# Block two's table products and their transfers at the end of a down projection instead of in the feed-forward loop

## The chip, the cores and the metric

The kernel runs on one core of a Trainium2 chip. The metric is the device time of one execution in microseconds; lower is better. Three runs of the kernel before gave 1399.70, 1400.94 and 1398.84 us, median 1399.7.

## What is computed

Two transformer blocks of two layers each run over one sequence of 256 positions and 1024 features, all in float32. Block one mixes by a gated recurrence (HGRN2) and by sparse attention (NSA), then a gated feed-forward. Block two mixes by attention with a relative bias, then a feed-forward with a convolution of width 3 over the positions. Cut to what the change touches:

```
def first_block(x, ...):
    for l in range(DEPTH):
        ...
        x = layer_norm(ALPHA * x + mix, ln1_g[l], ln1_b[l])
        ffn = (jax.nn.silu(x @ w_ffn_gate[l]) * (x @ w_ffn_up[l])) @ w_ffn_down[l]
        x = layer_norm(ALPHA * x + ffn, ln2_g[l], ln2_b[l])
    return x

def conv_ffn(h, w_up, conv_w, conv_b, w_down):
    u = h @ w_up
    up = jnp.pad(u, ((0, 0), (CONV_WIDTH - 1, 0), (0, 0)))
    c = conv_b
    for j in range(CONV_WIDTH):
        c = c + conv_w[j] * up[:, j:j + S]
    ...

def second_block(x, ..., rel_bias, ...):
    table_a = rel_bias[:, :A_HEADS].T
    table_b = rel_bias[:, A_HEADS:A_HEADS + B_HEADS].T
    for layer in range(DEPTH):
        h = rmsnorm(x, attn_norm[layer])
        ...
        l_own = jnp.where(d_own >= 0, l_own + table_hk[:, t5_bucket_2(d_own)], -jnp.inf)
        ...
        x = x + conv_ffn(h, w_up[layer], conv_w[layer], conv_b[layer], w_down[layer])
```

The moved step prepares two things for block two: the convolution's weights and bias with the features on partitions, and the relative bias laid out by distance.

## The kernel before

The 256 positions are two token blocks of 128 ("tb" 0 and 1). A weight is loaded by SyncE (SP) into one of four buffers "raw", 512 KB at a time; ScalarE (ACT) rounds it into "whi" (line 122), and VectorE (DVE) or GpSimd (POOL) writes the rest, "wlo" (line 128). A product is three matmuls: high with high, high with low, low with high (`mm3`, line 137; line 135 is every matmul, line 143 every transpose). PSUM has eight banks under four names: acc 3, S 2, T 2, O 1.

Each engine does its instructions strictly in its own order. That order is not the one in which the code is written: a planner orders what the code records, by the recorded place as priority and by what is ready on its own estimate of time, and `issue_after` and `high_priority` bend it. SP and POOL also have their transfers in this order: an issue that must wait holds up what stands behind it on the same engine.

`block2_tables` (line 487) is the moved step. For each layer of block two it loads the three taps and the bias of the convolution (44 rows) into a tile "sg", transposes them by four matmuls into PSUM and evacuates them into "taps". Then `rel_rows` (line 174) does, for "ev" (the first layer of block two) and "od" (the second):

- SP loads `c_rel` (33 x 384) into "sg"; one product gives the bias of 16 heads by distance; ACT evacuates it into another "sg" tile;
- POOL writes that row to HBM, "relrow" (line 190, 24 KB), waits until it has landed, and issues four copies "relrep" (line 196), each of which repeats the rows of four heads 128 times, 768 KB.

The tag "sg" has two buffers, which the feed-forward loop uses too. `load_bias` (line 208) later reads "relrep" into the tables tb2a and tb2b, at the start of each layer of block two.

`layer1` (line 499) is a layer of block one. Its feed-forward loop (line 554) runs over eleven column groups of 256, and has the moved step in front of the fifth group of the second layer. Then `proj_out` (line 294) does the down projection. At its end the second token block's last products stand, and a last piece of them, `rest`, is kept back for `handover` (line 403): the seam to block two. There the layer norm and the RMS norm of token block 0 run on DVE, ACT and POOL (`layer_norm` line 333, `rms_rows` line 857); TensorE (PE) transposes the normalised rows ("xn", eight transposes into two S banks), does `rest` and the first products of block two for token block 0, and then the same again for token block 1. Each norm takes its reciprocal root "rs" from POOL (`rsqrt`, line 145). The weights of the seam are w_in_even; the second half of them, for the T banks, goes into the tiles "hT", where POOL subtracts every other piece.

Of the kernel before, what the change touches and what calls it, by code (L numbers as in the profile page):

```python
# [18 lines left out]
P = 128  # L19
S = 256  # L20
# [4 lines left out]
NF = D_FF // P  # L25
# [58 lines left out]
class Kern:  # L84
# [86 lines left out]
            sl = slice(k * 512, k * 512 + 512)  # L171
            self.nc.sync.dma_start(self.x[:, tb, sl], self.I["x"][0, tb * P:(tb + 1) * P, sl])

    def rel_rows(self, stage, small, names):

        nc, I = self.nc, self.I
        for name in names:
            key, nh, c0, w = {"b1": ("rel_bias", 8, 0, 384), "ev": ("rel_bias_2", 16, 0, 384),
                              "od": ("rel_bias_2", 16, 384, 384), "cmp": ("rel_bias", 8, 768, 512)}[name]
            rb = self.t(self.small, (33, 16), tag="rb", bufs=2)  # L180
            nc.gpsimd.memset(rb[32:33, :nh], 1.0)
            nc.sync.dma_start(rb[0:32, :nh], I[key])
            rel = stage((33, 512))
            nc.sync.dma_start(rel[:, :w], I["c_rel"][:, c0:c0 + w])
            ps = self.psum("T")
            self.mm(ps[:nh, :w], rb[:, :nh], rel[:, :w])
            sb = small((16, 512))
            self.act(sb[:nh, :w], ps[:nh, :w])
            dr = self.dram.tile([nh, w], F32, name="relrow_" + name)
            nc.gpsimd.dma_start(dr, sb[:nh, :w])  # L190

            reps = 15 if name == "cmp" else P
            dd = self.dram.tile([nh, reps, w], F32, name="relrep_" + name)
            ap = dr[:, :]
            for h in range(0, nh, 4):
                nc.gpsimd.dma_start(dd[h:h + 4], bass.AP(tensor=ap.tensor, offset=ap.offset + h * w, ap=[[w, 4], [0, reps], [1, w]]))
            self.relrow[name] = dd
# [289 lines left out]
    def block2_tables(self, fp):  # L487
        nc, I = self.nc, self.I
        for l in range(2):
            raw = self.t(fp, (2 * NF, 4, P), tag="sg", bufs=2)  # L490
            nc.sync.dma_start(raw[:, 0:3, :], I["conv_w_2"][l].rearrange("j (m p) -> m j p", p=P))
            nc.sync.dma_start(raw[:, 3, :], I["conv_b_2"][l].rearrange("(m p) -> m p", p=P))
            ps = self.psum("T", (P, 4, 2 * NF))
            for j in range(4):
                self.tr(ps[:, j, :], raw[:, j, :], 2 * NF)
            self.act(self.taps[:, l], ps)
        self.rel_rows(lambda sh: self.t(fp, sh, tag="sg", bufs=2), lambda sh: self.t(fp, sh, tag="sg", bufs=2), ("ev", "od"))

    def layer1(self, l, xT, accs):
        nc, I, tc = self.nc, self.I, self.tc  # L500
        w = I["w_in"][l]
        mix = self.new_xT()
        with ExitStack() as st:
            hp = st.enter_context(tc.tile_pool(name="hg", bufs=1))
            self.pl = 0.5
            vv = self.t(hp, (P, 2, 512), tag="hv")
            for tb in range(2):
                self.act(vv[:, tb, :], accs[0][tb])
            fps = self.proj_a(w, 512, 512, xT)
            pcs = [self.wpiece(w[:, j * S:(j + 1) * S], NK, S, self.pl) for j in range(2)]  # L510
            lf, kk = self.hgrn_gates(l, fps, hp)
            qT = self.hgrn_q(w, xT, hp, pcs)
            kT = self.t(hp, (P, 4, S), tag="hkT")
            for tb in range(2):
                ps = self.psum("T", (P, 4, P))
                for h in range(4):
                    self.tr(ps[:, h, :], kk[:, tb, h * P:(h + 1) * P])
                nc.vector.tensor_copy(kT[:, :, tb * P:(tb + 1) * P], ps)
            if l == 0:
                self.hgrn_tables(hp)  # L520
            scs = [self.hgrn_scores(h, lf, kT, qT, hp) for h in range(4)]
            if l == 0:
                self.nsa_tables(hp)
            kv = self.nsa_keys(l, w, xT, hp)
            G = self.hgrn_g(l, w, xT, hp)
            for h in range(4):
                self.hgrn_out(l, h, scs[h], vv, G, mix, hp)
            nq = self.nsa_queries(w, xT, hp)
            self.nsa_attn(nq, kv, mix, hp)
            rows = [self.row(hp, I[key][l], D, tag) for key, tag in (("ln1_g", "lfh"), ("ln1_b", "lfl"))]  # L530
            self.pl = 0.5
            slots = self.slot_pairs(hp, [("hE", 2, 2)] * 2 + [(tag, 1, None) for tag in ("hkT", "hqT", "hv", "hG")])
            accs, rest = self.proj_out(I["w_out"][l], lambda k: (mix[0][:, k, :], mix[1][:, k, :]), [[0, 1, 2, 3], [4, 5, 6, 7]], slots)
            xT, (ga,) = self.handover(lambda tb: self.layer_norm(tb, accs[tb], rows), self.x, I["w_ffn_gate"][l],
                                      [(0, "acc", None)], rest)
            self.D(f"xa_{l}", self.x)
        with ExitStack() as st:
            fp = st.enter_context(tc.tile_pool(name="ffn", bufs=1))
            self.pl = 0.0
            rows = [self.row(fp, I[key][l], D, key) for key in ("ln2_g", "ln2_b")]  # L540
            hT = self.hidden(fp)

            ua = self.proj_a(I["w_ffn_up"][l], 0, 512, xT, "S")
            for tb in range(2):
                sg = self.t(fp, (P, 512), tag="sg", bufs=2)
                with tc.issue_after(self.after[0].ins):
                    self.act(sg, ga[tb], AF.Silu)
                nc.vector.tensor_tensor(sg, sg, ua[tb], ALU.mult)
                ps = self.psum("T", (P, 4, P))
                for k in range(4):  # L550
                    self.tr(ps[:, k, :], sg[:, k * P:(k + 1) * P])
                for c in range(2):
                    self.split(*[h[:, :, tb * P:(tb + 1) * P] for h in hT[c]], ps[:, 2 * c:2 * c + 2, :])
            for c in range(2, NF // 2):
                if l == 1 and c == 4:
                    self.block2_tables(fp)
                accs = []
                for key, tag in (("w_ffn_gate", "acc"), ("w_ffn_up", "S")):
                    accs.append(self.proj_b(I[key][l], c * S, S, xT, tag))
                sg = self.t(fp, (P, 2, S), tag="sg", bufs=2)  # L560
                self.act(sg, accs[0], AF.Silu)
                nc.vector.tensor_tensor(sg, sg, accs[1], ALU.mult)
                self.split(*hT[c], sg)
            args = self.hidden_args(fp, hT)
            self.pl = 0.0
            accs, rest = self.proj_out(I["w_ffn_down"][l], *args)
            norm = lambda tb: self.layer_norm(tb, accs[tb], rows)
            if l == 0:
                return self.handover(norm, self.x, I["w_in"][1], [(1024, "acc", None)], rest)
            return self.rms(fp, norm, I["attn_norm_2"][0], I["w_in_even_2"][0],  # L570
                            [(1024, "acc", None), (2560, "T", args[2])], rest)
# [535 lines left out]
```

## Time and profile before

| | before |
|---|---|
| median of 3 runs | 1399.7 us (1398.84 to 1400.94) |
| the profiled execution's own time | 1399.82 us |
| its span, first to last instruction | 1398.0 us |
| instructions | 24398 |
| busy: PE, PE weight loads, DVE, ACT, POOL | 98%, 87%, 70%, 58%, 21% |
| mean granted clock of PE | 0.993 of full speed |
| moved by DMA | 243.27 MB, mean 174 GB/s |

A profile is one execution. Its page gives the busy time of each engine and the chain of work that ended last. The trace behind it can be asked for a stretch: the instructions in order of time with the wait in front of each, the busy time of every engine by stretch, and the landing times of transfers. "<-" stands between what an instruction writes and reads. A row with x4 is four instructions that follow each other. The clock of PE is given as a share of 2.4 GHz.

### The profile page before, as it was taken

The page shows a single profiled execution, that of the slowest core. Times are in us where ns is not written, and L with a number is a line of the kernel's source. Part 1 is how long each engine was busy: PE and PEld are TensorE (multiplying, and loading weights), DVE is VectorE, ACT ScalarE, POOL GpSimd, SP SyncE. Part 2 cuts the span into 40 slices and gives each one's busy share as a digit, 9 for nine tenths or more (in the row PEclk, how much of TensorE's full clock was granted, in tenths as well). Part 3 has the DMA queues.
Part 4 walks back from the last instruction along what each step waited for, and adds up shares of the span by engine and source line. Part 5 has one row for each costly group of instructions (what it writes and reads, how often), then busy time and mean ns, then how long its engine had stood idle before and what let it go on. Part 6 is the DMA issues. An engine that isn't in the chain of part 4 may idle for free. (4 is left out here: it accounts for less than half of the span.)

```text
span 1398.0 us, 24398 instructions
## 1 busy us (share of the span) xinstructions
PE 1364.3 (98%) x8873; PEld 1210.2 (87%) x8873; DVE 979.7 (70%) x2006; ACT 813.9 (58%) x1623; POOL 299.8 (21%) x308
## 2 busy tenths in 40 slices
PE   8999999999999999999998998999999999999998
PEld 7788689998788967999887997799988988899986
DVE  5579675554877877655476699678866666688864
ACT  5466645554475574555454676577655577676653
POOL 3265210000234532020014545200001323100000
PEclk9999999999999999999999999999999999999999
DMA  8564155665655434689564654266556744456552
GB/s 267 159 208 151 61 180 170 184 187 170 198 151 172 121 106 131 206 242 292 181 210 136 222 150 152 78 195 190 187 183 200 240 144 155 153 172 184 186 187 100
DMA packets 188923, 243.27 MB, mean 174 GB/s; under 512 B 15551, under 2 KB 133346, under 8 KB 188803
## 3 DMA queue, kind: packets, MB, share of 16 engines
q1 hardware_dynamic: 179987, 228.22, 52.8%
q0 software_dynamic: 8816, 13.50, 2.9%
q8 instruction: 70, 1.15, 0.3%
q14 instruction: 50, 0.41, 0.1%
HBM read 240.49 MB, written 9.24 MB: 179 GB/s over the span
## 5 line engine op out<-in xcount | busy, mean ns | idle before, releaser
L128 DVE TENSOR_TENSOR wlo<-raw,whi 128x512 fp32r<-128x512 f32 (+2 forms) x619 | 458.3, 752 | 265.7 <-ACT whi L122 199.7
L122 ACT ACTIVATE whi<-raw 128x512 fp32r<-128x512 f32 (+1 forms) x742 | 454.6, 626 | 317.8 <-PE T L135 90.5
L128 POOL TENSOR_TENSOR wlo<-raw,whi 128x512 fp32r<-128x512 f32 (+2 forms) x123 | 172.0, 1403 | 656.3 <-ACT whi L122 654.9
L135 PE MATMUL acc<-xhi,whi 128*128 128x256 f32 x1048 | 298.2, 285 | 5.3 <-ACT whi L122 5.3
L135 PE MATMUL acc<-xlo,whi 128*128 128x256 f32 x1048 | 298.4, 285 | 0.0
L135 PE MATMUL acc<-xhi,wlo 128*128 128x256 f32 x1048 | 298.2, 285 | 0.0
L135 PEld LDWEIGHTS acc<-xhi,whi 128*128 128x128 f32 x1048 | 200.9, 192 | 7.7 <-ACT whi L122 5.9
L135 PEld LDWEIGHTS acc<-xhi,wlo 128*128 128x128 f32 x1048 | 200.8, 192 | 1.9 <-issue 0.6
L135 PEld LDWEIGHTS acc<-xlo,whi 128*128 128x128 f32 x1048 | 201.0, 192 | 1.5 <-issue 0.2
L135 PE MATMUL S<-xhi,whi 128*128 128x256 f32 x608 | 172.2, 283 | 0.0
L135 PE MATMUL S<-xlo,whi 128*128 128x256 f32 x608 | 172.2, 283 | 0.0
L135 PE MATMUL S<-xhi,wlo 128*128 128x256 f32 x608 | 172.1, 283 | 0.0
L135 PEld LDWEIGHTS S<-xhi,wlo 128*128 128x128 f32 x608 | 116.7, 192 | 0.6 <-DVE wlo L128 0.6
L135 PEld LDWEIGHTS S<-xlo,whi 128*128 128x128 f32 x608 | 116.7, 192 | 0.0
L135 PEld LDWEIGHTS S<-xhi,whi 128*128 128x128 f32 x608 | 116.7, 192 | 0.0
L135 PE MATMUL acc<-whi,xhi 128*128 128x512 f32 (+1 forms) x272 | 106.2, 396 | 1.7 <-ACT whi L122 1.7
L135 PE MATMUL acc<-wlo,xhi 128*128 128x512 f32 (+1 forms) x272 | 107.1, 394 | 0.2 <-DVE wlo L128 0.2
L135 PE MATMUL acc<-whi,xlo 128*128 128x512 f32 (+1 forms) x272 | 106.9, 395 | 0.0
L135 PE MATMUL acc<-whi,hT 128*128 128x512 f32 x288 | 95.6, 393 | 0.0
L122 ACT ACTIVATE ssb<-ssb,nmx 128x128 f32<-128x128 f32 (+1 forms) x128 | 57.0, 447 | 16.3 <-DVE nmx L372 15.5
L135 PEld LDWEIGHTS acc<-whi,hT 128*128 128x128 f32 x288 | 54.0, 188 | 12.4
L146 POOL TENSOR_TENSOR rs<-ve,mhalf 128x1 f32<-128x1 f32 x18 | 14.7, 818 | 228.8 <-DVE ve L866 208.4
(459 smaller groups left out, 2388.3 us busy)
## 6 DMA issues: line engine op xcount, KB each, us to landing
raw<-in_w_up_dram SPq DMA_DIRECT2D x88, 512.0 KB, 4.3
raw<-in_w_in_dram SPq DMA_DIRECT2D x46, 512.0 KB, 4.4
raw<-in_w_ffn_gate_dram SPq DMA_DIRECT2D x44, 512.0 KB, 3.9
raw<-in_w_ffn_up_dram SPq DMA_DIRECT2D x44, 512.0 KB, 4.4
raw<-in_w_ffn_down_dram SPq DMA_DIRECT2D x44, 512.0 KB, 4.5
raw<-in_w_down_dram SPq DMA_DIRECT2D x44, 512.0 KB, 4.0
raw<-in_w_in_even_dram SPq DMA_DIRECT2D x32, 512.0 KB, 4.3
raw<-in_w_in_odd_dram SPq DMA_DIRECT2D x24, 512.0 KB, 4.1
```

The source lines that it names most:

```text
L122: return self.nc.scalar.activation(out, in_, func, **k)
L128: b = (eng or self.nc.vector).tensor_tensor(lo, src, hi.bitcast(F32), ALU.subtract)
L135: return self.nc.tensor.matmul(out, lhsT=lhsT, rhs=rhs, start=start, stop=stop)
L146: self.nc.gpsimd.tensor_tensor(out, in_, self.mhalf[:, :n], ALU.pow)
```

## The change

The call of `block2_tables` goes from the fifth column group of the loop to behind `proj_out`, in front of the handover. Its PSUM tiles, of the transposes and of the rel products, come from the two S banks instead of the two T banks, since the down projection holds the T banks by then.

```diff
-    def rel_rows(self, stage, small, names):
+    def rel_rows(self, stage, small, names, tag="T"):
...
-            ps = self.psum("T")
+            ps = self.psum(tag)
             self.mm(ps[:nh, :w], rb[:, :nh], rel[:, :w])
...
-            ps = self.psum("T", (P, 4, 2 * NF))
+            ps = self.psum("S", (P, 4, 2 * NF))
             for j in range(4):
                 self.tr(ps[:, j, :], raw[:, j, :], 2 * NF)
             self.act(self.taps[:, l], ps)
-        self.rel_rows(lambda sh: self.t(fp, sh, tag="sg", bufs=2), lambda sh: self.t(fp, sh, tag="sg", bufs=2), ("ev", "od"))
+        self.rel_rows(lambda sh: self.t(fp, sh, tag="sg", bufs=2), lambda sh: self.t(fp, sh, tag="sg", bufs=2), ("ev", "od"), "S")
...
             for c in range(2, NF // 2):
-                if l == 1 and c == 4:
-                    self.block2_tables(fp)
                 accs = []
...
             accs, rest = self.proj_out(I["w_ffn_down"][l], *args)
+            if l == 1:
+                self.block2_tables(fp)
```

On PE, at the end of the down projection of the second layer, in the changed program (sg_8048 and sg_8057 hold the taps, sg_8069 and sg_8085 hold c_rel for ev and od, xn_8098 the normalised rows):

```order
L135 MATMUL O_7569<-hT_7968,hT_6162 128x512
L143 MATMUL S_8051<-ident,sg_8048 128x44 x4
L143 MATMUL S_8060<-ident,sg_8057 128x44 x4
L135 MATMUL S_8071<-sg_8069,rb_8066 16x384
L135 MATMUL S_8087<-sg_8085,rb_8082 16x384
L143 MATMUL S_8175<-ident,xn_8098 128x128 x4
```

In the program before, the transposes of xn follow directly on the down projection's product into O; the tap transposes and the two rel products now stand between.

On POOL, at the same place, in the program before (from the last weight piece ahead of the norms to the second block's RMS norm):

```order
L128 TENSOR_TENSOR wlo_8144<-raw_8137,whi_8143 128x512
L146 TENSOR_TENSOR rs_8171<-ve_1640_8169,mhalf 128x1
L128 TENSOR_TENSOR hT_8196<-raw_8189,hT_8195 128x512
L128 TENSOR_TENSOR hT_8206<-raw_8199,hT_8205 128x512
L128 TENSOR_TENSOR hT_8216<-raw_8209,hT_8215 128x512
L146 TENSOR_TENSOR rs_8289<-ve_8287,mhalf 128x1
L128 TENSOR_TENSOR hT_8226<-raw_8219,hT_8225 128x512
L146 TENSOR_TENSOR rs_8304<-ve_1671_8302,mhalf 128x1
```

and in the changed program:

```order
L128 TENSOR_TENSOR wlo_8144<-raw_8137,whi_8143 128x512
L190 DMA relrow_ev<-sg_8073 16x384
L196 DMA relrep_ev<-relrow_ev 512x1x384 x4
L146 TENSOR_TENSOR rs_8171<-ve_1640_8169,mhalf 128x1
L190 DMA relrow_od<-sg_8089 16x384
L128 TENSOR_TENSOR hT_8196<-raw_8189,hT_8195 128x512
L128 TENSOR_TENSOR hT_8206<-raw_8199,hT_8205 128x512
L196 DMA relrep_od<-relrow_od 512x1x384 x4
L128 TENSOR_TENSOR hT_8216<-raw_8209,hT_8215 128x512
L128 TENSOR_TENSOR hT_8226<-raw_8219,hT_8225 128x512
L146 TENSOR_TENSOR rs_8289<-ve_8287,mhalf 128x1
L146 TENSOR_TENSOR rs_8304<-ve_1671_8302,mhalf 128x1
```

The ten transfers stood ahead of the seam, in the feed-forward stage; now five stand in front of the first block's rs (rs_8171) and five between it and the second block's two (rs_8289, rs_8304).

On SP, in the changed program, behind the loads of the seam's weights:

```order
L228 DMA raw_8209<-in_w_in_even_dram 128x2x512
L228 DMA raw_8219<-in_w_in_even_dram 128x2x512
L184 DMA sg_8069<-in_c_rel_dram 33x384
L184 DMA sg_8085<-in_c_rel_dram 33x384
L228 DMA raw_8395<-in_w_in_even_dram 128x8x80
```

The two loads of c_rel stood among those of w_ffn_gate and w_ffn_up before; the loads of the taps and the bias now stand among the first of w_ffn_down.

## Rows read from the trace of the kernel before

**Rows 1.** The page's first part: busy time and share of each engine.

```profile
PE 1364.3 (98%) x8873; PEld 1210.2 (87%) x8873; DVE 979.7 (70%) x2006; ACT 813.9 (58%) x1623; POOL 299.8 (21%) x308
```

**Rows 2.** Busy time by stretch, in the feed-forward stage; its columns first.

```profile
core 0: us, PE busy (x) PEld busy (x) DVE busy (x) ACT busy (x) POOL busy (x), PEclk, DMA share, GB/s
...
614.00:626.00 12.00, 12.00 (x102) 12.00 (x102) 4.99 (x8) 4.52 (x8) 0.00 (x0) 1.00 1.04 313
```

**Rows 3.** Instructions of PE in order of time, feed-forward stage: start, duration, what.

```profile
596.28 0.28 PE L135 MATMUL acc<-xhi,whi 128*128 128x256 f32 x1
596.50 0.44 PE L143 MATMUL T<-ident,sg 44*128 44x44 f32 x4
596.87 0.39 PE L135 MATMUL acc<-xlo,whi 128*128 128x256 f32 x1
...
598.40 0.28 PE L135 MATMUL S<-xlo,whi 128*128 128x256 f32 x1
598.61 0.82 PE L135 MATMUL T<-sg,rb 33*16 33x384 f32 x2
599.36 0.39 PE L135 MATMUL S<-xhi,wlo 128*128 128x256 f32 x1
```

**Rows 4.** The same of PE in the seam: the transposes of both token blocks.

```profile
738.46 1.94 PE L143 MATMUL S<-ident,xn 128*128 128x128 f32 x8 [3.98 <-DVE xn L872]
...
754.24 1.07 PE L143 MATMUL S<-ident,xn 128*128 128x128 f32 x8 [0.38 <-DVE xn L872]
```

**Rows 5.** Busy time by stretch in the seam, and SP's eighth load of w_in_even.

```profile
738.46:743.99 5.53, 5.53 (x17) 4.71 (x18) 4.07 (x5) 4.24 (x9) 2.35 (x2) 0.50 0.11 43
743.99:754.24 10.25, 9.87 (x44) 7.73 (x42) 9.34 (x15) 2.71 (x7) 5.23 (x5) 1.00 0.69 186
...
735.90 0.37 SPq L228 DMA_DIRECT2D raw<-in_w_in_even_dram  x1
```

**Rows 6.** Instructions of POOL in order of time, in the seam.

```profile
737.25 0.55 POOL L146 TENSOR_TENSOR rs<-ve,mhalf 128x1 f32<-128x1 f32 x1 [3.22 <-DVE ve L866]
741.64 4.70 POOL L128 TENSOR_TENSOR hT<-raw,hT 128x512 fp32r<-128x512 f32 x3 [3.84 <-ACT hT L122]
747.34 0.92 POOL L146 TENSOR_TENSOR rs<-ve,mhalf 128x1 f32<-128x1 f32 x1 [1.00 <-DVE ve L344]
...
753.02 0.55 POOL L146 TENSOR_TENSOR rs<-ve,mhalf 128x1 f32<-128x1 f32 x1 [3.35 <-DVE ve L866]
...
767.39 0.95 POOL L212 DMA_DIRECT2D tb2a<-relrep_ev  x1 [1.13 <-PE T L135]
```

**Rows 7.** The same of POOL in the feed-forward stage: all that it does there.

```profile
600.51 0.60 POOL L190 DMA_DIRECT2D relrow_ev<-sg  x1 [53.13 <-ACT sg L122]
604.12 4.34 POOL L196 DMA_DIRECT2D relrep_ev<-relrow_ev  x4 [3.02 <-DMA relrow_ev<-sg]
608.45 0.52 POOL L190 DMA_DIRECT2D relrow_od<-sg  x1
626.37 4.33 POOL L196 DMA_DIRECT2D relrep_od<-relrow_od  x4 [17.39 <-DMA relrow_od<-sg]
```

**Rows 8.** DMA issues of the whole execution: KB each, median us to landing.

```profile
relrep_b<-relrow_b POOLq DMA_DIRECT2D x2, 768.0 KB, 12.4
...
hE<-in_c_mask_dram SPq DMA_DIRECT2D x1, 256.0 KB, 3.2
...
rb<-in_rel_bias_dram SPq DMA_DIRECT2D x2, 2.0 KB, 1.5
kirow<-in_idx_k_norm_dram SPq DMA_DIRECT2D x1, 32.0 KB, 5.1
```

**Rows 9.** Landing times of block one's two copies and of tb.

```profile
DMA to landing us min/median/max: 6.8/10.9/13.8
```

**Rows 10.** An instruction of DVE in the seam: the layer norm's last step, second token block.

```profile
750.15 1.40 DVE L350 SCALAR_TENSOR_TENSOR x<-x,rs,ln_b 128x512 f32<-128x512 f32 x2
```

**Rows 11.** The chain that ended last, in order of time: the first use of tb2b.

```profile
845.97 1.23 DVE db L998
```

## The prediction

> **What bounds the kernel now.** I read the page first, then the stretch around the old place of the tables, then the stretch around the new one. The page says that TensorE is busy 98% of the span [rows 1], so the kernel is a nearly unbroken line of matmuls, and a change pays or costs by the time it puts into that line or takes out of it.
>
> The old place is the second layer's feed-forward stage. Between 614 and 626 us, while the tables' copies are in flight, the DMA engines are busy to 1.04 at 313 GB/s, and TensorE is still busy for all 12.00 us with 102 instructions [rows 2]. The copies therefore slow down no matmul there. What the tables cost there is their own few matmuls.
>
> The new place is the seam behind the down projection. TensorE stands still there for 3.98 us before the eight transposes of the first token block at 738.46, waiting for VectorE's xn, and for 0.38 us before those of the second block at 754.24 [rows 4]. I call the start of the first of these waits R: 738.46 - 3.98 = 734.48, where the last down-projection product ahead of the transposes ends. All times with a plus below are counted from R. The first transposes stand at +3.98, the second at +19.76. What releases both is a chain that goes over POOL: the reciprocal root "rs" of the RMS norm at 737.25, that of the second block's layer norm at 747.34 and of its RMS norm at 753.02 [rows 6].
>
> **What the stage gives back.** Four groups leave the feed-forward stage. In the row of matmuls there one starts every 0.12 us; between the starts at 596.28 and 596.87 lie 0.59 us, so one group of four tap transposes costs 0.47; between 598.40 and 599.36 lie 0.96, so one rel product costs 0.84 [rows 3]. Twice both is 2.6 us saved. The small evacuations and loads that leave with them were hidden behind TensorE and give nothing.
>
> **What the seam gets: the first wait.** By the order of instructions TensorE now runs eight tap transposes, then the two rel products, and only then the first block's transposes. The tap transposes take 0.9 us and lie in the 3.98 us of idleness; their tables were loaded during the down projection, beside matmuls. The first rel product needs c_rel. Its load is issued by SP behind the eighth load of w_in_even, which goes out at 735.90 and takes 0.37 to issue [rows 5], so c_rel goes out at +1.8. Its time to landing is not shown. The nearest loads are 1.5 us (2 KB), 3.2 (256 KB) and 5.1 (32 KB, in busy queues) [rows 8]; c_rel has 49.5 KB, and I take 3.2, with 1.5 and 5.1 as the ends. The product starts at +5.0.
>
> From that product to the moment when POOL has issued the four ev copies, the rows of before give the whole chain (evacuation, relrow written, its landing waited for, four issues): 598.61 to 608.45, 9.84 us [rows 3, 7]. POOL stands in this chain with all of its queue, and the first block's rs is queued right behind the fourth issue. So rs starts at +14.8 instead of +2.8, although its input is ready well before. From rs to the transposes it is 738.46 - 737.25 = 1.21 [rows 4, 6], so these start at +16.0. The od product (c_rel again, after the first product) and its evacuation on ACT lie beside this, while POOL issues. The first block is **12.1 us late**.
>
> **The second wait.** Behind rs POOL issues relrow_od, does two subtractions of weight pieces, and then waits until relrow_od has landed before it may issue the four od copies. Behind these stand the other two subtractions and the second block's rs. In the old place the same wait took 17.39 us, with POOL having nothing else to do, because the 24 KB row came back only after the ev copies of 4 x 768 KB ahead of it [rows 7]. How long that takes in the seam is the largest unknown. The first ev copy is issued 604.12 - 598.61 = 5.5 us after the product, at +10.5, the fourth three quarters of 4.34 later, at +13.8. With few weights in flight the block-one copies of the same size landed in 10.9 and 13.8 us, median 12.4 [rows 8, 9]; with the full stream the od row was back 22.25 after the first ev issue [rows 7]. SP has little in flight here, because the raw buffers are held until POOL's subtractions are done; so I take 12.4: the row lands at +26.2 (ends: +24.7 and +32.8). Then come four issues, 4.33 [rows 7], two subtractions at 4.70/3 = 1.57 each, rs 0.92 [rows 6], and from the layer norm's last step on VectorE to the transposes 754.24 - 750.15 = 4.09 [rows 4, 10]: 12.5 in all, so the second block's transposes start at +38.7. They stood at +19.76. The second block, and with it everything behind, is **18.9 us late**, the first wait included.
>
> The Trainium skill speaks against the change where it says to issue a transfer early, compute, and wait for it late (DMA: Bandwidth & Descriptors, Rules for kernel authors); here issue and wait are moved next to each other. Its own price for this is a fixed cost of about 2 us a transfer (same page, Latency and other measured facts); by that the two small transfers of the first wait would cost about 2.2 us less than by my rows and the sum would be 1416.7.
>
> **The clock.** After the 3.98 us of idleness the granted clock is 0.50, which is 1.2 GHz, for the 5.53 us from 738.46, and 1.00 (2.4 GHz) after that; the 0.38 us before the second transposes brought no fall [rows 5]. At half clock 5.53 us of work lose 2.8. In the change TensorE has 15.78 us of work from +16.0 on [rows 4], in which it also waits for POOL's late subtractions, so it stands still for some 7 us in all before +38.7. I expect a second such stretch: **2.8 us**; the ends are 0 and 2.8. The first stretch is there before and after.
>
> **What costs nothing.** The tb2 loads that read the copies are issued at 767.39 and the first table is needed at 845.97 [rows 6, 11]: some 78 us of slack against a delay of the od copies ahead of them. The first loads of the next projection stand behind c_rel on SP, but they wait longer for raw buffers anyway. If that cover is gone, weights come late in the even projection; I count that only in the upper end.
>
> **The sum.** -2.6 + 18.9 + 2.8 = +19.1 us. The profiled execution took 1399.82 us, span 1398.0, and lies 0.1 above the median of the runs, 1399.7. So 1399.8 + 19.1 = **1418.9**. About 0.2% (2.8 us) is what a measurement of this kernel can tell from no change.
>
> **Rivals.** *Only the first wait.* If the od row landed by +19.3, POOL would be through in time and the second block would stand 15.78 behind the first, as before: 12.1 - 2.6 = +9.5, 1409.3. Against it: that is 5.5 us after the fourth ev issue, and the fastest such copy shown took 10.9.
>
> *The copies run at full rate.* With the weight stream nearly at rest, the ev copies' 3.15 MB at the 313 GB/s of the stage [rows 2] take 10.1 us, the row lands at +20.6, the second block is 20.6 + 12.5 - 19.8 = 13.3 late, and with the clock and the saving the sum is +13.5: 1413.3. Against it: the block-one copies, two of them and not four, took 10.9 to 13.8 each. The Trainium skill has a rule to this effect: all queues' transfers run on the same 16 engines and interleave (DMA: Bandwidth & Descriptors, Issuing engines are not separate DMA queues), so a silent queue leaves its share to the other.
>
> *The copies are as slow as in the stage.* 22.25 us from the first ev issue puts the row at +32.8 and the sum at -2.6 + 25.5 + 2.8 = +25.7: 1425.5. For it speaks the pure copy of the row; against it the thinner stream.
>
> *Faster.* The tables' chain could be hidden in the idle 3.98 us if POOL had issued the ev copies by +2.8, when rs wants to run. Then only the saving is left: -2.6, 1397.2. For that the product would have to start 7 us before R, and it stands behind the down projection in TensorE's order. That decides it, and leaves little chance.
>
> **How the numbers follow.** Forecast 0.64; first wait only 0.10; full rate 0.12; slow copies 0.12; faster 0.02. The time is the forecast's. The range, 1409 to 1427, reaches from the first-wait case to the slow copies with the longer c_rel landing. By these cases: faster by over 0.2% 0.02, within 0.2% 0.02, slower 0.96.
>
> **What would show it.** In the profile of the change TensorE should wait about 16 us around the first transposes, in two pieces with the rel products between them, and again before the second ones, in the end for VectorE's xn. POOL's rs should follow the fourth ev issue at once, and relrep_od should wait for the DMA of relrow_od by some 4 us behind two subtractions. The feed-forward stage should be 2.6 us shorter. The forecast is wrong if rs runs ahead of the copies, if the od row is back at once, or if the even projection waits for weights.

## The result and the profile after

The changed kernel takes 1416.94 us, median of four runs (1416.50 to 1417.34), against 1399.27 for the kernel before, median of four on the same chip. The ratio is 1.0127, with a 95% interval of 1.0114 to 1.014: slower by 17.7 us. The forecast was +19.1. The profiled execution took 1417.34 us, its span is 1415.3.

The first part of the page of the changed kernel, which answers to [rows 1]:

```profile
PE 1366.6 (97%) x8873; PEld 1210.7 (86%) x8873; DVE 977.2 (69%) x2006; ACT 814.4 (58%) x1623; POOL 296.4 (21%) x308
```

The work is the same. TensorE is busy 2.3 us longer, in a span that is 17.3 us longer, so some 15 us of the loss are TensorE standing still. Where it stands, the timeline of PE in the seam shows (it answers to [rows 4]):

```profile
729.37 0.69 PE L143 MATMUL S<-ident,sg 44*128 44x44 f32 x8
734.78 1.44 PE L135 MATMUL S<-sg,rb 33*16 33x384 f32 x2 [4.72 <-DMA sg<-in_c_rel_dram]
738.02 1.44 PE L135 MATMUL S<-sg,rb 33*16 33x384 f32 x2 [1.81 <-DMA sg<-in_c_rel_dram]
744.77 1.94 PE L143 MATMUL S<-ident,xn 128*128 128x128 f32 x8 [5.31 <-DVE xn L872]
...
762.38 0.80 PE L135 MATMUL T<-hT,xhi 128*128 128x512 f32 x1 [4.61 <-POOL hT L128]
...
768.22 1.94 PE L143 MATMUL S<-ident,xn 128*128 128x128 f32 x8 [3.33 <-DVE xn L872]
```

From here on a plus ahead of a point in time counts from the start of the tap transposes, here 729.37, which follow the down projection without a pause; in the kernel before it counts from R. The first transposes of xn stand at +15.4 (before: +3.98), the second at +38.9 (before: +19.76). TensorE waits 4.72, 1.81, 5.31, 4.61 and 3.33 us.

The chain that ended last, in order of time, gives the reason for each of these waits (start, us, what):

```profile
731.30 3.35 DMA sg<-in_c_rel_dram
...
734.78 1.45 PE S L135 x2
...
736.25 0.49 ACT sg L122
...
737.03 1.86 DMA relrow_ev<-sg
...
739.18 1.55 POOL relrep_ev L196 x2
...
741.36 2.15 POOL relrep_ev L196 x2
...
743.53 0.53 POOL rs L146
744.06 12.33 DMA relrow_od<-sg
...
758.88 2.15 POOL relrep_od L196 x2
...
761.05 2.52 POOL hT L128 x2
763.57 0.52 POOL rs L146
...
768.22 1.94 PE S L143 x8
```

It is read from the top. One small load, the two small writes and between them the issues of the copies carry the seam as far as the second block's norm; the first rs (743.53) runs directly behind the fourth ev issue, the second block's (763.57) behind the od issues and two subtractions. None of the load, the writes and the issues is work of a norm. The longest piece is the landing of relrow_od, 12.33 us for 24 KB.

With TensorE's instructions matched one by one, the lag of the changed kernel behind the one before is (at times of the kernel before; plus and minus are only signs here): -2.4 us at 136 us, where both programs are still the same (executions differ by that much in their first 80 us); -2.1 at 580, just ahead of the old place; -5.0 behind it, up to the seam (the last six products into O start at 732.96 before and at 727.92 here); +6.3 at the first transposes; +14.0 at the second; +15.5 from 758 to 860 (the first product of the even projection starts at 766.92 before and at 782.43 here); +17.2 at the last matmul.

### The profile page after: what moved, and what is told of

Read it like the earlier page. It is cut to its first block, busy times and chain, and to the rows that moved or that the text cites. A ratio compares the mean times of both kernels' runs of the same rounds, so it can differ in the third digit from the quotient of the medians.

```text
span 1415.3 us, 24398 instructions
## 1 busy us (share of the span) xinstructions
PE 1366.6 (97%) x8873; PEld 1210.7 (86%) x8873; DVE 977.2 (69%) x2006; ACT 814.4 (58%) x1623; POOL 296.4 (21%) x308
## 4 chain that ended last, share of the span: by engine, by line
PE 54%; DVE 3%; DMA 2%; issue 2%; POOL 1%; ACT 1%; POOLq 0%; SPq 0%; DVEq 0%; ACTq 0%
PE acc L135 29%; PE S L135 15%; PE O L135 4%; PE T L135 4%; PE T L143 1%; DMA relrow_od<-sg 1%; DMA raw<-in_w_o_dram 1%; PE S L143 1%; DVE wlo L128 0%; DVE ssb L372 0%; DVE x L350 0%; POOL relrep_od L196 0%; POOL relrep_ev L196 0%; DMA sg<-in_c_rel_dram 0%; DVE x L349 0%
## 5 line engine op out<-in xcount | busy, mean ns | idle before, releaser
L135 PEld LDWEIGHTS acc<-whi,xhi 128*128 128x128 f32 x272 | 51.8, 191 | 11.3 <-ACT whi L122 1.7
```

Source lines behind the costliest of these rows:

```text
L135: return self.nc.tensor.matmul(out, lhsT=lhsT, rhs=rhs, start=start, stop=stop)
```

## Experiments

The theory: the loss is a matter of queues. POOL's queue holds the copies' issues and a wait ahead of rs; what is left is TensorE's own queue, in which the rel products with a late c_rel stand ahead of the transposes. Rival A: the traffic of the copies slows the seam wherever it is issued. Rival B: the added work of TensorE and ACT is what costs. Rival C: a single one of the two waits sets the end. In the table "first" and "second" are the transposes of the two token blocks; medians of before are those taken beside each run.

| run | first | second | median us | before | ratio, 95% |
|---|---|---|---|---|---|
| the change | +15.4 | +38.9 | 1416.9 | 1399.3 | 1.0127 [1.0114, 1.014] |
| od_stays | +6.9 | +25.0 | 1404.5 | 1400.7 | 1.0034 [1.0018, 1.005] |
| ev_stays | +7.1 | +25.2 | 1404.7 | 1399.0 | 1.0048 [1.0026, 1.007] |
| taps_only | +5.4 | +21.1 | 1399.2 | 1400.7 | 0.9996 [0.9977, 1.0015] |
| crel_early | +9.7 | +28.5 | 1408.0 | 1400.7 | 1.0059 [1.004, 1.0077] |
| copies_sp | +10.4 | +26.4 | 1445.3 | 1400.7 | 1.0331 [1.0297, 1.0365] |
| sp_128 | +10.5 | +26.5 | 1404.7 | 1399.9 | 1.004 [1.0026, 1.0055] |
| pool_128 | +14.2 | +34.7 | 1413.9 | 1399.9 | 1.0102 [1.0085, 1.012] |
| norms_first | +10.8 | +26.7 | 1407.2 | 1398.7 | 1.0068 [1.0052, 1.0085] |
| copies_behind | +5.5 | +21.2 | 1403.6 | 1398.7 | 1.0038 [1.0023, 1.0054] |
| mid_tables | | | 1410.4 | 1398.7 | 1.008 [1.0066, 1.0094] |
| early_tables | | | 1410.0 | 1398.7 | 1.0082 [1.0068, 1.0095] |
| back_to_back | | | 1402.1 | 1399.0 | 1.0019 [1.0005, 1.0034] |

### One group at the seam, the other in the old place: od_stays, ev_stays

```diff
-        self.rel_rows(..., ("ev", "od"), "S")
+        self.rel_rows(..., ("ev",), "S")
...
+                if l == 1 and c == 4:
+                    self.rel_rows(..., ("od",))
```

The second run has ev and od exchanged.

> The taps and ev at the seam as in the change, od left in the feed-forward stage. By the order of instructions POOL now has the first block's rs ahead of relrow_ev, and nothing of od behind it. Theory (what delays the seam is what stands in POOL's and PE's queues): first transposes right behind the ev product, at +6.9 from the end of the down projection instead of +15.4; POOL then waits some 2 us for relrow_ev, issues for 4.3 us and does four subtractions, so rs of the second block comes at about +21 and the second transposes at about +26 (19.8 before, 38.8 in the change); -1.8 saved, 6.4 lost, 1.2 clock: about 1405. Rival (the copies' traffic delays the seam's weights and norms wherever they are issued): ev's copies are half of it, so about half of the 17.7 us, 1408 to 1412, with waits on DMA of raw. Rival (PE's and ACT's extra work is what costs): the same, nearly unchanged 1415.

> The mirror of the run that left od in the stage: ev stays in the feed-forward stage, the taps and od go to the seam. By the order of instructions POOL has the first block's rs, then relrow_od, the wait for it, the four od copies, four subtractions and the second block's rs. Theory (the od row came back late in the change only because the four ev copies stood ahead of it): with nothing ahead relrow_od lands in some 2 us as the ev row did, POOL waits 1.5 us for it, first transposes at +6.9, second at +25, time as in the mirror, 1403 to 1406. Rival (the od row is slow by itself, or the seam's traffic holds it): a wait of 6 us or more behind relrow_od, second transposes at +30 or more, 1408 to 1412.

Both came out as the theory has it. The timeline of POOL with od left in the stage:

```profile
735.25 0.54 POOL L146 TENSOR_TENSOR rs<-ve,mhalf 128x1 f32<-128x1 f32 x1 [4.54 <-DVE ve L868]
738.85 0.56 POOL L190 DMA_DIRECT2D relrow_ev<-sg  x1 [3.06 <-ACT sg L122]
740.95 4.34 POOL L196 DMA_DIRECT2D relrep_ev<-relrow_ev  x4 [1.54 <-DMA relrow_ev<-sg]
```

and with ev left there:

```profile
740.87 4.34 POOL L196 DMA_DIRECT2D relrep_od<-relrow_od  x4 [1.54 <-DMA relrow_od<-sg]
```

With nothing ahead of it the od row costs the same wait of 1.54 us as the ev row. In the change it took 12.33 us to land because the four ev copies were ahead of it: the last of them, issued at 742.44, took 13.8 us and so landed at 756.2, and the row landed at 756.4. One group at the seam costs 4 to 6 us by the medians, both together 17.7: the second group does not add its own price, it adds the landing of the first. Rival C falls with the change's own lag: it grows by 11.3 us up to the first transposes and by another 7.7 between these and the second, and neither is made good later.

### Only the taps at the seam: taps_only

```diff
-        self.rel_rows(..., ("ev", "od"), "S")
...
+                if l == 1 and c == 4:
+                    self.rel_rows(..., ("ev", "od"))
```

> Only the tap transposes at the seam, both rel products and all copies in the feed-forward stage. Theory: nothing of it is in POOL's queue, so no wait on POOL; the stage gives back 0.9 us, and the two evacuations into taps on ACT stand ahead of the squares and hold these up by some 0.9 us: 1398.4 to 1399.3, first transposes at +4 to +5. Rival (tap loads and the S banks are part of the loss): 1402 or more.

No difference from before. The second transposes are 1.3 us later than in the kernel before, which eats the 0.9 us that the stage gives back. The expectation puts such a delay down to the two evacuations in front of the squares on ACT. The trace shows another step: the squares are done at 736.15 and xn's first step at 736.52, but VectorE then does two steps of the second block's layer norm (736.44 to 737.84) ahead of the one that rs waits for (ve, 737.76); in the kernel before ve comes first, at 736.97. So for the taps Rival B is at most this small: TensorE's idle time hides the eight transposes. copies_behind, below, has the two products as well.

### c_rel loaded early: crel_early

```diff
+            rb, rel = early.get(name) or self.rel_load(key, nh, c0, w, stage)
...
+                if l == 1 and c == 4:
+                    self.early = {...}
```

`rel_load` holds the two loads that stood here; `early` is filled in the feed-forward stage, in buffers of its own.

> As the change, but c_rel for ev and od is loaded in the feed-forward stage into buffers of its own. Theory: the ev product starts at +0.7 instead of +5.4, the whole POOL chain moves ahead by about 5 us: first transposes at +10 (5.9 late), od row back at about +22, second transposes at +33 (13.6 late); about 1411.5. Rival (the landing of c_rel is beside the path, the chain is set by the copies alone): 1416 to 1417. Rival (the first wait alone sets the end): 1403 to 1405.

The first transposes came where expected, the second 4.5 us sooner than expected, and the time lies 3.5 us below the expected 1411.5. The planner had also changed POOL's order, which the expectation did not allow for, as POOL's timeline shows:

```profile
732.11 0.60 POOL L195 DMA_DIRECT2D relrow_ev<-sg  x1 [2.86 <-ACT sg L122]
733.23 0.50 POOL L195 DMA_DIRECT2D relrow_od<-sg  x1 [0.52 <-ACT sg L122]
735.83 2.22 POOL L201 DMA_DIRECT2D relrep_ev<-relrow_ev  x2 [2.11 <-DMA relrow_ev<-sg]
738.07 0.57 POOL L146 TENSOR_TENSOR rs<-ve,mhalf 128x1 f32<-128x1 f32 x1
...
747.30 1.08 POOL L201 DMA_DIRECT2D relrep_od<-relrow_od  x1 [3.17 <-issue]
```

Both rows are written ahead of any copy, so there is no wait for the od row at all. In its place the eighth copy is held for 3.17 us. The profile names no releaser, but the landing times do: the first copy, issued at 735.83, took 11.1 us and so landed at 746.9, and the eighth goes out at 747.30. Both changes act here, and this run does not part them.

### The copies issued by SP: copies_sp, and walked the other way: sp_128, pool_128

```diff
-            nc.gpsimd.dma_start(dr, sb[:nh, :w])
+            q = nc.sync if tag == "S" else nc.gpsimd
+            q.dma_start(dr, sb[:nh, :w])
...
-                nc.gpsimd.dma_start(dd[h:h + 4], ...)
+                q.dma_start(dd[h:h + 4], ...)
```

> As the change, but all ten transfers relrow and relrep of ev and od are issued by SP instead of POOL. Theory (POOL's queue): rs no longer waits; what is left is PE's order, where both rel products with c_rel landing late stand ahead of the transposes: first transposes at about +10.7 and the second 15.8 behind, 6.7 late instead of 18.9; with -2.6 and 1.2 for the clock about 1405; SP now holds its weight loads behind the od row until about +27, which may come late for the even projection and would show as PE waits on whi there (up to 1410). Rival (the copies' traffic, or PE's order, is the cause and not POOL's queue): second transposes at +35 or more, 1413 to 1417.

The seam did what the theory says, and the whole did not. PE, in order of time:

```profile
740.15 2.12 PE L143 MATMUL S<-ident,xn 128*128 128x128 f32 x8 [0.18 <-DVE xn L873]
756.08 1.07 PE L143 MATMUL S<-ident,xn 128*128 128x128 f32 x8 [0.62 <-DVE xn L873]
774.40 0.50 PE L135 MATMUL acc<-xhi,whi 128*80 128x256 f32 x1 [5.48 <-ACT whi L122]
810.96 0.58 PE L135 MATMUL acc<-xhi,whi 128*128 128x256 f32 x1 [31.13 <-ACT va L122]
```

With POOL free, the second transposes stand at +26.4 instead of +38.9: 12.5 of the 19.1 us between before and the change belong to POOL's queue. The other 6.6 belong to the late c_rel, and not over TensorE's queue alone, as the theory has it. There the transposes stand behind the od product, which starts at +8.8 and ends at 739.98. But they then wait another 0.18 us for xn, and xn is late because of ACT's queue:

```profile
736.63 0.48 ACT L122 ACTIVATE sg<-S 16x384 f32<-16x384 f32 x1 [5.87 <-PE S L135]
737.14 0.60 ACT L122 ACTIVATE S<-x 128x512 f32<-128x512 f32 x1
```

The squares of the RMS norm (S<-x) stand behind the evacuation of the ev product, though their x is ready by 730.5. By these times either queue alone would hold the transposes to about the same point. But the next weights stand behind the copies on SP, and those run slowly. Busy time by stretch, while the ev copies are under way (the last two numbers are the share of 16 DMA engines and GB/s):

```profile
744.00:756.00 12.00, 11.46 (x47) 8.97 (x46) 11.17 (x16) 4.49 (x10) 6.91 (x6) 0.95 0.26 99
```

A share of 0.26 is that of four engines of 16. I had costed SP's copies like POOL's; the next two runs test this.

```diff
+                dst, src = dd[h:h + 4], [[w, 4], [0, reps], [1, w]]
+                if name in ("ev", "od"):
+                    dst, src = dst.rearrange("a r w -> r a w"), [src[1], src[0], src[2]]
```

> As the run with SP as issuer, but each copy is walked with its 128 repetitions outermost and the four heads inside (128x4x384 instead of 4x128x384); the bytes and their places are the same. That run moved only 100 GB/s at a DMA share of 0.26 while SP's copies were under way. Theory (a copy whose outermost dimension is 4 keeps 4 of the 16 DMA engines busy, and on SP's queue always the same ones, so its weights stood behind 31 us of copies): at some 300 GB/s the ev copies take 10 us, the od row is back at +19, the waits of 5.48 and 31.13 us for weights go; the seam stays 6.7 late: 1404 to 1410. Rival (SP's queue is slow for copies from HBM to HBM as such, or the short pieces of 1.5 KB set the rate): 1435 to 1447.

> The change itself with the same new walk of the copies, POOL issuing. Theory: on POOL's queue the four copies of a group were already spread over all engines (DMA share 1.05 at 310 GB/s between 746 and 752), so the od row comes back no sooner than 10 us after its issue and the time stays 1414 to 1417. Rival (the narrow copies start slowly, each on four engines, and wide ones get the full rate from the first on): od row back 4 to 5 us sooner, second transposes at +34, 1411 to 1413.

With SP as issuer the time falls from 1445.3 to 1404.7 by this alone. The same stretch of its copies, and its PE at the second transposes:

```profile
746.00:756.00 10.00, 10.00 (x44) 8.12 (x43) 9.97 (x15) 3.23 (x8) 5.65 (x5) 0.96 1.07 308
```

```profile
757.36 1.07 PE L143 MATMUL S<-ident,xn 128*128 128x128 f32 x8 [0.51 <-DVE xn L876]
```

The Trainium skill has the rule (DMA: Bandwidth & Descriptors, Why a DMA increments its semaphore by 16 and not by 1, and Rules for kernel authors): the outermost dimension sets how many of the 16 engines a transfer uses, those of SP and ACT being always the lowest-numbered, those of POOL consecutive ones from a moving start. The trace agrees on the number: 0.26 of the engines and 99 GB/s for 4 outermost, 1.07 and 308 for 128; which engines they are, no view here shows.

Rival A falls here: the second transposes stand at +26.5 with the DMA engines at 1.07 and at +26.4 with them at 0.26, so four times the copies' rate does not move them. And pool_128, below, differs from sp_128 in nothing but the issuer of the ten transfers: 1413.9 against 1404.7, so to have them in POOL's queue costs 9.2 us.

On POOL the gain is small, but it lies between theory and rival: the ratio is 1.0102 against 1.0127 for the change, and the second transposes come 4.2 us sooner. The landing of its copies (KB each, median us to landing):

```profile
relrep_ev<-relrow_ev POOLq DMA_DIRECT2D x4, 768.0 KB, 9.3
...
relrow_od<-sg POOLq DMA_DIRECT2D x1, 24.0 KB, 10.7
```

against 13.2 and 12.3 in the change. Busy time by stretch from 1.8 us behind the first ev issue on, first the change, then pool_128:

```profile
741.00:744.00 3.00, 0.00 (x0) 0.00 (x0) 0.00 (x0) 0.00 (x0) 2.98 (x4) 0.50 0.45 114
```

```profile
744.50:747.50 3.00, 0.52 (x3) 0.56 (x4) 0.49 (x1) 0.72 (x1) 2.41 (x4) 0.50 0.99 307
```

Between 746 and 752 us the change too is at 1.05 and 310 GB/s. So the four narrow copies of a group did spread over the engines, but not from the first moment on. POOL also issues a wide copy in 0.75 us, not 1.08.

### The copies behind the norms: norms_first, copies_behind

```diff
+        self.lastrs = self.nc.gpsimd.tensor_tensor(out, in_, self.mhalf[:, :n], ALU.pow)
...
+                if l == 0:
+                    with tc.issue_after(self.lastrs.ins):
+                        self.copies["ev"]()
+                self.kz[1:] = [self.key_pair(hp, f"b{l}", nc.gpsimd)]
...
+            if l == 0:
+                with tc.issue_after(self.lastrs.ins):
+                    self.copies["od"]()
```

`copies` keeps the four issues of a group for later; the second run has c_rel early as well.

> As the change (taps, both products, both evacuations and both relrow writes at the seam, c_rel loaded there too), but POOL issues the ev copies only behind the second block's rs, and the od copies in the first feed-forward stage of block two; tb2 is loaded behind POOL's memsets. Theory (the loss is the place of the copies' issues and of their wait in POOL's queue, beside PE's own order): no wait of POOL is left in front of rs; PE's order stays (ev and od product with late c_rel ahead of the transposes): first transposes at +10.4, second at +26.4 as where SP issued the copies, that is 6.7 late; -2.6 + 6.7 + about 1 for the clock: 1404.5, 1403 to 1406. Rival (traffic of the copies beside the first weights of block two): 1410 or more, with PE waits on raw in the even projection.

> The same with c_rel loaded early in the feed-forward stage, so that both products run by +2.3. Theory: what is left at the seam are two evacuations of taps and two of rel on ACT ahead of or between the squares, and two relrow issues on POOL: first transposes at about +6 (2 late), second at about +22 (2.3 late); against 2.6 given back: 1399 to 1400, no change that can be measured against before. Rival (the products as such are a loss at the seam, or the copies' traffic): 1403 or more. Rival (the filled idle time keeps the clock up and saves the half-clock stretch of before): 1396 to 1397.

At the seam both are as forecast, within 1 us: with POOL's queue freed +10.8 and +26.7, with c_rel early +5.5 and +21.2. So queue positions and the two late loads together account for all but 1.4 us of the second block's delay, and the work that was moved (Rival B) for no more than these 1.4. The times are not as forecast: 2.7 us above the expected 1404.5, and 3.6 above the upper end of 1399 to 1400. The larger part is shown: the od copies now run beside the first weights of block two's feed-forward, ACT waits for a weight there, and TensorE stands (first of the two runs, ACT and PE):

```profile
923.88 1.15 ACT L122 ACTIVATE whi<-raw 128x512 fp32r<-128x512 f32 x2 [8.73 <-DMA raw<-in_w_up_dram]
...
929.63 0.33 PE L143 MATMUL T<-ident,ua 128*128 128x128 f32 x1 [2.01 <-ACT ua L122]
```

In the kernel before it does not stand at all between 905 and 940 us. The lag grows there by 2.6 us in the first run and by 3.7 in the second. In both runs POOL also holds an issue of tb2b, with memsets of the next tables behind it, for 3.38 us in the first and in the second for 4.17:

```profile
769.85 0.91 POOL L223 DMA_DIRECT2D tb2b<-relrep_ev  x1 [4.17 <-issue]
```

In the stretch behind it, up to 800 us, the lag grows by 0.9 and 1.8 us; which of the transfers and memsets there costs this stays open. The profiled execution of the second run, 1400.68, lies near the lower end of its seven: it was already 4.6 us ahead of the kernel before at 80 us, where the programs are the same, and falls back by 5.4 from there to its end.

### Other places for the tables: mid_tables, early_tables, back_to_back

From the kernel before, with the eight copies issued together in the second layer's feed-forward stage behind its last rs:

```diff
+            if l == 1:
+                self.block2_tables(hp)
             scs = [self.hgrn_scores(h, lf, kT, qT, hp) for h in range(4)]
...
-                    self.block2_tables(fp)
+                    with tc.issue_after(self.lastrs.ins):
+                        for copies in self.copies.values():
+                            copies()
```

The second run calls `block2_tables` behind `rel_rows` of the first layer instead.

> The kernel before, but the tables' loads, transposes, products and relrow writes stand in the second layer's recurrence, where TensorE has gaps of 1.48, 0.69, 0.46 and 0.56 us between 411 and 423 us, and the eight copies are issued by POOL in the feed-forward stage behind its last rs there. Theory (a product costs what it adds to TensorE's line, and nothing in a gap): up to 2.6 us given back, 1396.7 to 1398.5. Rival (ACT's four evacuations of 2 us lie on the path there): 1399.3 to 1401.

> The same with the tables in the first layer, in front of the gap of 5.27 us at 67 us in which TensorE waits for raw weights, and the copies in the second layer's feed-forward stage. Theory: the products vanish in the gap, 2.6 us given back: 1396.7 to 1397.5. Rival (the six small loads stand in SP's queue ahead of the weights that the gap waits for and lengthen it by their issue time, about 2 us): 1399 to 1400.

Both missed: some 11 us slower, by a cause that neither expectation names. The copies went out at the start of the stage. POOL and PE of the first run:

```profile
549.28 4.42 POOL L199 DMA_DIRECT2D relrep_ev<-relrow_ev  x4
553.68 3.23 POOL L199 DMA_DIRECT2D relrep_od<-relrow_od  x3
569.16 1.08 POOL L199 DMA_DIRECT2D relrep_od<-relrow_od  x1 [12.24 <-issue]
```

```profile
574.05 0.38 PE L135 MATMUL acc<-xhi,whi 128*128 128x256 f32 x1 [4.41 <-ACT whi L122]
```

The weights came late there: ACT's rounding of whi, for which TensorE waits, had itself waited 14.15 us for a load of w_ffn_gate. DMA issues from 540 to 580 us of this run, and then the same of the kernel before:

```profile
raw<-in_w_ffn_up_dram SPq DMA_DIRECT2D x4, 512.0 KB, 18.3
raw<-in_w_ffn_gate_dram SPq DMA_DIRECT2D x4, 512.0 KB, 12.1
```

```profile
raw<-in_w_ffn_gate_dram SPq DMA_DIRECT2D x6, 512.0 KB, 4.2
raw<-in_w_ffn_up_dram SPq DMA_DIRECT2D x5, 512.0 KB, 5.3
```

TensorE stands still for 6.05 us between 545 and 600 in both runs, before for none. The eighth copy is held again until the first has landed (549.28 + 19.5 = 568.8). In the first run the lag behind the kernel before also grows in the recurrence, from -1.7 us at 400 to +1.9 at 510. That says nothing of the tables: in pool_128, which has the program of before there, it grows from -2.1 us to +1.3 over the same stretch. What the tables cost in the recurrence and in the first layer stays open.

The last run asks whether the old place has room because the copies go out in two groups:

```diff
+        with self.tc.issue_after(self.lastrow.ins):
+            for copies in self.copies.values():
+                copies()
```

> The kernel before, with the tables in their old place, but both relrow writes issued before any copy, so that POOL issues the eight copies of 768 KB in one row and not in two groups 22 us apart. Theory (the 17.39 us wait behind relrow_od in the kernel before spreads the copies, and the stage's weight stream has room for four copies at a time but not for eight): PE waits for whi appear some 15 to 30 us after the first copy, 3 to 8 us in all, 1402 to 1407. Rival (the stage in its middle has room for all eight, and only its start, where the weight buffers run empty behind the norms, has none): 1398 to 1400 as before.

Between the two: the time is at the lower end of the theory's range, and TensorE's waits are shorter than its 3 to 8 us. Busy time by stretch:

```profile
620.00:630.00 10.00, 10.00 (x85) 10.00 (x85) 3.29 (x6) 3.56 (x7) 0.00 (x0) 1.00 1.11 337
630.00:640.00 10.00, 9.77 (x81) 9.54 (x80) 4.38 (x7) 3.70 (x7) 0.00 (x0) 1.00 1.05 341
640.00:650.00 10.00, 9.13 (x74) 8.72 (x74) 7.39 (x12) 6.67 (x13) 0.00 (x0) 1.00 0.83 247
```

TensorE begins to stand, 1.1 us in all, where it stood for none in the kernel before, and over these waits the lag grows by 2.0 us. Of the 0.19% (2.7 us) no more than these 2.0 are shown to be the copies'. None of the twelve versions beats the kernel before.

## Why the prediction was right

By its own steps, with what the trace of the change and the runs showed.

- **What the stage gives back**, 2.6: the lag falls from -2.1 to -5.0 over the old place, 3.0. Right, and a little under-sized.
- **The first wait**, 12.1: 11.3 by the lag (+6.3 against -5.0). c_rel was issued at +1.9 and the product ran at +5.4 (said: +1.8 and +5.0), rs at +14.2 (+14.8), directly behind the fourth ev issue. The rows of before carried the steps of this chain to the new place, but not all of its length: from the product to rs it took 8.75 us (743.53 - 734.78) where 9.84 was said, since relrow_ev was back sooner than in the stage. The two small transfers landed in 3.35 us (c_rel, issued 0.4 us behind a weight load on the same queue) and 1.86 us (relrow_ev); the Trainium skill's fixed cost of about 2 us (DMA: Bandwidth & Descriptors, Latency and other measured facts) fits the second and not the first. That the 1416.7, which the prediction works out by this price, lies next to the time measured is therefore chance. One thing was missed: rs's input too is late. ACT's squares stand behind the evacuation of the ev product in the change as well (736.77 behind 736.25), and ve, which rs waits for, comes at 738.28, that is +8.9 and not some +2.8; it is still 5.3 us ahead of rs. The od product, which the prediction rightly has beside POOL's issues, ran at +8.7, since the second c_rel goes into a buffer that the first product has to free. In the change POOL's queue hides both; once POOL is free, they hold the transposes, and so the 6.6 us of copies_sp.
- **The second wait**, from 12.1 to 18.9 late: 19.0 by the lag (+14.0 against -5.0). The od row was back 17.5 us after the first ev issue (756.68 - 739.18; said: 15.7). That is nearer to the forecast than to the rivals on the copies' rate, 10.1 and 22.25, which both fell; pool_128 shows that part of the gap to the full rate is the copies' narrow shape (14.5 us there). The first ev issue came at +9.8 where +10.5 was said, and the way from the row to the transposes took 11.5 us where 12.5 was said: 1.8 too late, 0.7 and 1.0 too early. The mechanism is as forecast; that the size fits to 0.1 us is luck.
- **The rival with the first wait alone** fell: it needs the od row back by +19.3, and POOL could go on at +27.3 (756.68).
- **The clock**, 2.8: this term was mis-sized. The second stretch at half clock is there, but short (busy time by stretch, the clock is the number ahead of the DMA share):

```profile
744.77:748.40 3.63, 3.63 (x15) 3.26 (x16) 1.71 (x3) 2.34 (x6) 0.45 (x1) 0.62 0.87 295
...
762.38:764.90 2.52, 2.50 (x5) 1.49 (x5) 0.79 (x2) 0.00 (x0) 1.70 (x2) 0.50 0.78 266
768.22:771.50 3.28, 3.28 (x12) 2.99 (x13) 1.37 (x2) 1.28 (x3) 0.00 (x0) 0.51 1.05 351
```

  The 2.5 us at 762 lie in time that TensorE would have waited anyway; of the 3.28 us behind the second transposes, which in the kernel before ran at full clock, the lag shows 1.5 us (from +14.0 to +15.5). I had copied the length of the first stretch, 5.53 us.
- **What costs nothing**: right. TensorE is busy for all 18.5 us from 771.5 to 790 us and for all 70 us behind that, so no weight of the even projection came late.
- **The signs**: TensorE's waits around the first transposes are 11.8 us and not about 16, in three pieces, since the od product lies between them as well; relrep_od waits 5.72 us for its row and not some 4.
- **Left over**: the lag grows by another 1.7 us behind 860 us, in block two's sparse attention and later, where the program is the same. Of it 1.3 us lie between 860 and 900 us, where every other run matched in this way falls back by 0.6 to 2.0 us against the kernel before too, so that this is no effect of the change. With the -2.4 of the start, and 0.4 by which the lag grows from there to the old place, it nearly cancels: -2.4 + 0.4 - 3.0 + 11.3 + 7.7 + 1.5 + 1.7 = 17.2, the lag of the last matmul (the spans differ by 17.3). The three terms of the forecast alone make -3.0 + 19.0 + 1.5 = 17.5 where 19.1 was said: the clock was 1.3 too high, the stage's gift 0.4 too low.

## What to carry to other kernels

Before moving a step, list what its instructions will stand in front of on each queue, the issues of transfers included: here a 24 KB write that had to land before the next issue cost as much as the four copies in flight ahead of it, and it cost that to all who waited behind it on the same engine. Look at the engines that evacuate as well as at the one that issues: here ACT's squares stood behind an evacuation that waited for a late load. An idle gap on the busiest engine is no free place if the gap is the wait for a chain that uses the queue into which the step is put. And look for a stage that has room for the transfers: in two groups the eight copies cost TensorE no wait in the middle of the feed-forward stage, and at its start, all in a row, 6 us; four of them at the start of another such stage cost 2 us.

## What the runs showed of the hardware that I had not expected

- A copy with 4 outermost, issued by SP, moved at 99 GB/s with a DMA share of 0.26; with 128 outermost, the same bytes at 308 GB/s and 1.07. That was worth 40 us here (copies_sp against sp_128).
- POOL held the eighth copy of 768 KB in each run that issued eight in a row, for 3.17, 12.24, 12.25 and 4.49 us (crel_early, mid_tables, early_tables, back_to_back), and let it go some 0.4 us after the first had landed. Seven were under way in each of them. A plain count of transfers it is not: in norms_first and copies_behind tb2b was held with only tb2a and one or two copies under way, and went out some 0.5 us after the last copy had landed (758.97 + 17.5 = 776.5 against 777.03, and 751.00 + 18.3 = 769.3 against 769.85). What the limit counts stays open.
